# Recurrence, norms and the up-phase seam of a hybrid trunk layer: pinned program order, later scaling, other engines for some splits

## The chip, the core and the metric

The kernel is one program on one core of one Trainium2 chip. The core has five engines that run at once: TensorE (matmuls and transposes; PE in the profile, PEld its weight loads), VectorE (DVE), ScalarE (ACT), GpSimd (POOL) and SyncE (SP, which here only issues DMAs). The metric is device time of one execution in microseconds, as the median of three runs.

## The reference

One layer of a decoder trunk, for a sequence of 1024 tokens of width 1024, in float32:

```python
h = rms_norm(x, norm1_g); proj = h @ w_in
p_rwkv, p_sb, q_mem, gate_logits = split(proj)
y_a = rwkv7_branch(p_rwkv)        # 8 heads x 64: a recurrence over the tokens, then a norm per head
y_b = stick_breaking_branch(p_sb) # 8 heads x 64
y_m = memory_branch(q_mem, mem)   # 4 heads x 128
branch_out = einsum('btnc,ncd->btnd', stack(y_a, y_b, y_m), w_branch)
merged = sum_n sigmoid(gate_logits[n]) * branch_out[n]
x = x + merged @ w_out
x = x + conv_ffn(rms_norm(x, norm2_g))  # up (2 x 2816), causal conv of width 3, silu * value, down
```

In the recurrence each step does `S = S * w + (S @ -kk) (kk * a) + v k` and `y = S @ r`. The norm per head takes the mean and variance over the 64 channels of y.

## The kernel before

Every large product is made of three float32r matmuls: an operand is split into a high part (a rounding copy, on ScalarE) and a low part (operand minus high, on VectorE or GpSimd), and the product is high x high + high x low + low x high. `mm3` issues the three, `split_raw` makes the two parts of a weight (its low part on GpSimd, L81), `product` does the same for the up-projection.

Instructions are ordered on each engine by a scheduler, except where `pinned` is called while `self.pin` is set: `keep_in_program_order` puts such an instruction behind the instruction of the same engine that the code issued before it. TensorE's matmuls and transposes are all pinned there. Tiles come from pools with a fixed number of buffers, so a load into a new tile waits until the old tile's last reader is done.

The recurrence (`stage2`, about 812 to 1028 us) works in 16 chunks of 64 tokens, four pairs of heads each. A chunk has three steps, with a `yield` behind each: v1 from the state (copied from PSUM by VectorE, L527), w (copied by ScalarE, L535), and then y (ScalarE, L547, into the tiles `qk`) and the new state U (VectorE, L545; U and v1 share the tile `ys`). At each `yield` other work is woven in between: `gate_item`, the gates' projections (copied out by ScalarE at L745, multiplied by the row factor `rbc` on VectorE at L746), and `branch_item`, the branches' products (multiplied by the gate on VectorE at L1146, added to the merged tile on GpSimd at L1148, stored to `mrd` at L1149). `load_y` loads a branch's four input tiles (`yd`), and `split_y` splits them (L1108 high, L1109 low).

At each chunk step `next(norm)` also advances `norm_part`, the head norm of the chunks that are done: sums (L568), squares on ScalarE (L575, into the scratch tile `jk`), the power -1/2 on GpSimd (`rsqrt`, L165 and L166), and the scaling of y in pieces of 64 columns on VectorE (L582). `group_norm` then transposes y (`turn`, L596 and L597) and splits it. `branch_last` makes the last branch's product and the merged activations, `out_proj` multiplies them by `w_out` (eight tiles of tokens, `tt`), adds x and takes the second norm (`norm`), and transposes it (`spread`).

The feed-forward's up-projection is a Strassen-like product of quarters: `sums` makes differences of quarters (L1275), and seven products use the operands 11, 21, 22, T1, T2, T3 and T4, each split by `high` (L1288) and `low` (L1293). Weights come in pairs of blocks; `hl` splits a weight (L1377, L1378), `prep2` and `prep3` first make sums of weights on GpSimd (L1394 to L1407). The first pairs, from the output projection's last tile to about 1250 us, are the seam, whose order is written out by hand at the end of `up_phase`.

Of the kernel before, what the change touches and what calls it, by code (L numbers as in the profile page):

```python
# [49 lines left out]
class Trunk:  # L50
# [111 lines left out]
    def rsqrt(self, out, ss, n, scale, eps):  # L162
        nc = self.nc
        t = self.small("rs", [128, 16])
        nc.vector.tensor_scalar(t[:, :n], ss, scale, eps, ALU.mult, ALU.add)  # L165
        nc.gpsimd.tensor_tensor(out, t[:, :n], self.half[:, :n], ALU.pow)  # L166
# [305 lines left out]
    def stage2(self):  # L472
# [33 lines left out]
        for c in range(NC):  # L506
# [16 lines left out]
            for p, h2 in heads:  # L523
                _, _, _, M, wv, _, v1, pb = us[p]
                self.mmul(pb[hq[h2], A], M[hq[h2], h2 * 128 + 64 : h2 * 128 + 128], wv[h2][hq[h2]], start=(c == 0), stop=True)
                if h2 == 1:
                    nc.vector.tensor_copy(v1, pb[:, A])  # L527
# [11 lines left out]
            for p, (Up, ra, bt, M, wv, tt, v1, pb) in enumerate(us):  # L539
                for h2, q in enumerate(hq):  # L540
                    self.mmul(pb[q, Y], M[:, h2 * 128 : h2 * 128 + 64], wv[h2], start=(c == 0), stop=True)
                if c < NC - 1:
                    for h2, q in enumerate(hq):
                        self.mmul(pb[q, S], bt[:, q], wv[h2], start=True, stop=True)
                    nc.vector.scalar_tensor_tensor(Up, Up, self.pc[p][:, c : c + 1], pb[:, S], ALU.mult, ALU.add)  # L545
                for h2, q in enumerate(hq):
                    nc.scalar.activation(self.y[p][cc * 64 : cc * 64 + 64, g * 128 + h2 * 64 : g * 128 + h2 * 64 + 64], pb[q, Y], AF.Copy)  # L547
# [5 lines left out]
            if c in (3, 7, 11, 13, 15):  # L553
                for _ in norm:
                    pass
                norm = self.norm_part(*{3: (0, 2), 7: (2, 4), 11: (4, 6), 13: (6, 7), 15: (7, 8)}[c])
            if c == 13:
                self.gs = [self.load_gg(p) for p in range(2)]
        for _ in norm:
            pass  # L560

    def norm_part(self, g0, g1):
# [8 lines left out]
        groups = [[(y[:, j * 64 : (j + 1) * 64], p * nh + j) for j in range(nh)] for p, y in enumerate(ys)]  # L571
        for gs in groups:
            for y, j in gs:
                junk = self.small("jk", [128, 80], bufs=1)[:, :64]
                nc.scalar.activation(junk, y, AF.Square, bias=nm[:, j : j + 1], accum_out=vs[:, j : j + 1])  # L575
            yield
        rs = self.small("hf", [128, 16], bufs=4)
        self.rsqrt(rs[:, : 4 * nh], vs[:, : 4 * nh], 4 * nh, 1.0 / 64, 64e-5)
        yield
        for gs in groups:  # L580
            for y, j in gs:
                nc.vector.tensor_scalar(y, y, nm[:, j : j + 1], rs[:, j : j + 1], ALU.add, ALU.mult)  # L582
            yield

    def group_norm(self):
# [5 lines left out]
        def turn(p, h, eng):  # L591
# [5 lines left out]
            eng.tensor_tensor(y[:, hs], gg[:, hs], bg[:, hs], ALU.add)  # L597
# [7 lines left out]
        for p in range(4):  # L605
            turn(p, 0, nc.vector)
            if p % 2:
                yield
# [492 lines left out]
    def split_y(self, ys):  # L1101
        nc = self.nc
        hi = self.pool_a.tile([128, 4, 1024], F32R, name=self.nm("yhi"), tag="inst")
        his = [hi[:, k] for k in range(4)]
        out = []
        for hi, y in zip(his, ys):
            lo = self.t4("A", F32R)
            nc.scalar.activation(hi, y, AF.Copy)  # L1108
            nc.vector.tensor_tensor(lo, y, hi.bitcast(F32), ALU.subtract)  # L1109
            out.append((hi, lo))  # L1110
        return out

    def load_y(self, b):
        ys = []
        for k in range(4):
            y = self.t4("w4")
            self.nc.sync.dma_start(y, self.yd[b, k])
            ys.append(y)
        return self.split_y(ys)
# [5 lines left out]
    def branch_item(self, b, d, st, first):  # L1125
# [21 lines left out]
        if not first:  # L1147
            nc.gpsimd.tensor_tensor(g, g, o, ALU.add)  # L1148
# [3 lines left out]
    def branch(self, b, first):  # L1152
        st = {}

        def load():
            st["y"] = self.load_y(b)

# [5 lines left out]
        return load, items  # L1163
# [6 lines left out]
    def branch_last(self):  # L1170
# [7 lines left out]
        rest = []  # L1178
        for d in range(8):
            if d % 2 == 0:  # L1180
                w = self.split_w(self.I["w_br"][0, d // 2])
            g, o = self.t4("at"), self.t4()
            nc.sync.dma_start(g, self.gsd[0, d])
            nc.sync.dma_start(o, self.mrd[d])
# [10 lines left out]
            if d in (2, 3, 4, 5, 6):  # L1195
                self.load_wo(d - 2)
# [19 lines left out]
    def out_proj(self):  # L1216
        nc = self.nc
        for k in range(5, 8):
# [19 lines left out]
        def norm(tt, pp):  # L1238
# [9 lines left out]
            rs = self.small("rs2", [128, 1])  # L1248
            self.pinned(nc.vector.tensor_tensor(rs, ss[:, 0:1], ss[:, 1:2], ALU.add))
            self.rsqrt(rs, rs, 1, 1.0 / D, 1e-6)  # L1250
# [35 lines left out]
        def high(name, src, ts=slice(0, 512)):  # L1286
            for j in range(2):
                self.pinned(nc.scalar.activation(self.B[name][0][j][:, :, ts], src[j][:, :, ts], AF.Copy))  # L1288

        def low(name, src, eng, ts=slice(0, 512)):  # L1290
            for j in range(2):
                hi, lo = self.B[name][0][j][:, :, ts], self.B[name][1][j][:, :, ts]
                self.pinned(eng.tensor_tensor(lo, src[j][:, :, ts], hi.bitcast(F32), ALU.subtract))  # L1293

        def split(*a):
            high(*a[:2], *a[3:])
            low(*a)
# [4 lines left out]
        def late(tt):  # L1302
            spread(tt, sqs.pop(tt))
            if tt == 3:
                for i in (0, 1):
                    operand(("11", "21")[i], self.pool_l, "l4")
                    split(("11", "21")[i], [halves(j)[i] for j in range(2)], nc.gpsimd)
            elif tt == 5:
                sums(0, 256)
            elif tt == 6:  # L1310
                sums(256, 384)

# [26 lines left out]
        for tt in range(2, 8):  # L1339
# [4 lines left out]
            sqs[tt] = norm(tt, pp)  # L1344
            if tt == 5:
# [6 lines left out]
    def up_phase(self, raws, t2, operand, high, low, late, sums):  # L1352
        nc = self.nc
        old, new = slice(0, 384), slice(384, 512)
        operand("T2", self.pool_r, "T2", bufs=4)
        operand("T1", self.pool_l, "l4")
# [10 lines left out]
        def load(n):  # L1367
            if n < len(pairs):
                tag, m = ("rw", pairs[n][0]) if n % 2 == 0 else ("wr", pairs[n][0])
                pool = self.pool_r if n % 2 == 0 else self.pool_wt  # L1370
# [4 lines left out]
        def hl(src, pool, tags, n=1024):  # L1375
            hi, lo = (pool.tile([128, n], F32R, name=self.nm(t), tag=t, bufs=16 if t == "l4" else 2) for t in tags)
            nc.scalar.activation(hi, src, AF.Copy)  # L1377
            nc.gpsimd.tensor_tensor(lo, src, hi.bitcast(F32), ALU.subtract)  # L1378
# [7 lines left out]

        def prep2(n):
            if n == 0:
                w = self.early[1]
            else:  # L1390
# [500 lines left out]
```

## Time and profile before

| | |
|---|---|
| median of 3 runs | 1851.92 us (1851.91 to 1853.56) |
| the profiled execution | 1854.88 us, of which the span is 1853.1 us |
| mean granted TensorE clock | 0.992 |
| TensorE busy | 1793.0 us, 97% of the span |
| VectorE, ScalarE, GpSimd busy | 63%, 48%, 42% |

A row of the timeline gives the start, the length, the engine, the source line, what is written from what, and in square brackets the idle time of that engine before it with the event that ended it. A row of the windows gives for a stretch of time the busy time and count of each engine, then the clock that TensorE was granted, the share of DMA time and the GB/s.

### The profile page before, as it was taken

Reading aid. Unit: us, or ns where it says so; the run is one execution under the profiler, and the core shown is the slowest. Engines: PE = TensorE matmul, PEld = TensorE weight load, DVE = VectorE, ACT = ScalarE, POOL = GpSimd, SP = SyncE. Lnnn points to the kernel's source line nnn. Section 1 sums busy time; section 2 is a strip of 40 time slices with the busy share of each in tenths; the row PEclk is TensorE's granted clock in tenths of the full one; section 3 lists DMA queues with packets and bytes.
Section 4 is the critical chain, followed back from the end, with each engine's and each line's share of the span. In section 5 each row is a group of like instructions: output and inputs, shape, how many; then the busy total and the mean of one; then the engine's idle time right before and its main releaser. Section 6 shows DMA issues by size and latency. Waiting matters only on the chain. (4 is left out here: it accounts for less than half of the span.)

```text
span 1853.1 us, 27444 instructions
## 1 busy us (share of the span) xinstructions
PE 1793.0 (97%) x10468; PEld 1448.0 (78%) x10468; DVE 1171.0 (63%) x1654; ACT 880.9 (48%) x1665; POOL 783.6 (42%) x449
## 2 busy tenths in 40 slices
PE   8999999999999999998989999979999999999999
PEld 6777778878788887786767778768888888878877
DVE  5657664998987414323434682477776777885596
ACT  5443343555666635534536443454454444454433
POOL 2322343232222452112323350477776767545454
PEclk9999999999999999999999999999999999999999
DMA  4155465111112442558654462323232233395475
GB/s 179 58 170 182 160 205 183 49 42 53 52 53 76 123 129 78 180 207 274 215 188 179 174 235 103 114 68 108 93 123 92 95 116 108 120 324 204 142 243 189
DMA packets 120613, 263.39 MB, mean 142 GB/s; under 512 B 28313, under 2 KB 40857, under 8 KB 120354
## 3 DMA queue, kind: packets, MB, share of 16 engines
q1 hardware_dynamic: 82722, 194.76, 32.2%
q10 hardware_dynamic: 33984, 54.27, 8.0%
q0 software_dynamic: 3776, 12.62, 2.1%
q8 instruction: 82, 1.34, 0.3%
q14 instruction: 49, 0.40, 0.1%
HBM read 180.04 MB, written 81.53 MB: 141 GB/s over the span
## 5 line engine op out<-in xcount | busy, mean ns | idle before, releaser
L81 POOL TENSOR_TENSOR wl<-wr,wh 128x1024 fp32r<-128x1024 f32 x77 | 195.9, 2545 | 486.4 <-ACT wh L80 482.3
L112 PE MATMUL mm<-xhi,wh 128*128 128x512 f32 x784 | 265.8, 420 | 9.4 <-ACT xhi L179 7.5
L112 PE MATMUL mm<-xlo,wh 128*128 128x512 f32 x784 | 246.9, 396 | 0.9 <-DVE xlo L180 0.9
L112 PE MATMUL mm<-xhi,wl 128*128 128x512 f32 x784 | 244.6, 394 | 0.2 <-POOL wl L81 0.2
L112 PEld LDWEIGHTS mm<-xlo,wh 128*128 128x128 f32 x784 | 149.6, 191 | 35.1 <-DVE xlo L180 1.6
L112 PEld LDWEIGHTS mm<-xhi,wl 128*128 128x128 f32 x784 | 148.7, 190 | 34.4 <-POOL wl L81 1.1
L112 PEld LDWEIGHTS mm<-xhi,wh 128*128 128x128 f32 x784 | 138.5, 192 | 39.9 <-issue 9.1
L80 ACT ACTIVATE wh<-wr 128x1024 fp32r<-128x1024 f32 x77 | 81.4, 1057 | 144.6 <-PE mm L112 85.5
L112 PE MATMUL mm<-dw,da 128*128 128x512 f32 x528 | 121.5, 390 | 2.3 <-DVE da L1631 2.1
L112 PE MATMUL mm<-BT,l 128*128 128x512 f32 x504 | 117.9, 389 | 0.5 <-POOL l L1378 0.5
L112 PEld LDWEIGHTS mm<-dw,da 128*128 128x128 f32 x528 | 98.8, 188 | 24.3 <-DVE da L1631 3.4
L1632 POOL TENSOR_TENSOR dw<-draw,dw 128x512 fp32r<-128x512 f32 x55 | 81.4, 1488 | 83.5 <-ACT dw L1630 82.1
L112 PEld LDWEIGHTS mm<-BT,l 128*128 128x128 f32 x504 | 94.5, 188 | 20.5 <-POOL l L1378 1.0
L844 DVE TENSOR_TENSOR_SCAN at<-at,at 128x128 f32<-128x128 f32 (+3 forms) x64 | 93.3, 1459 | 26.6 <-ACT at L838 26.4
L112 PE MATMUL mm<-BT,wh 128*128 128x512 f32 x352 | 108.8, 390 | 0.7 <-DVE u L1430 0.7
L112 PE MATMUL mm<-B,wh 128*128 128x512 f32 x352 | 108.5, 389 | 0.0
L1631 DVE TENSOR_TENSOR da<-draw,da 128x512 fp32r<-128x512 f32 x77 | 65.7, 863 | 59.0 <-ACT da L1629 58.4
L112 PE MATMUL g<-dw,da 128*128 128x512 f32 x396 | 90.9, 390 | 2.2 <-ACT dw L1630 1.1
L1378 POOL TENSOR_TENSOR l<-it,l 128x1024 fp32r<-128x1024 f32 x21 | 50.8, 2418 | 92.3 <-ACT l L1377 92.3
L112 PEld LDWEIGHTS g<-dw,da 128*128 128x128 f32 x396 | 74.3, 188 | 18.4 <-ACT dw L1630 1.6
L1629 ACT ACTIVATE da<-draw 128x512 fp32r<-128x512 f32 x77 | 48.3, 628 | 83.3 <-PE mm L112 39.5
L746 DVE TENSOR_TENSOR w<-w,rbc 128x1024 f32<-128x1024 f32 x24 | 48.7, 2029 | 61.8 <-ACT w L745 61.8
(324 smaller groups left out, 3994.3 us busy)
## 6 DMA issues: line engine op xcount, KB each, us to landing
wr<-in_w_in_dram SPq DMA_DIRECT2D x50, 512.0 KB, 3.6
draw<-actd SPq DMA_DIRECT2D x77, 256.0 KB, 3.4
at<-scr SPq DMA_DIRECT2D x28, 512.0 KB, 6.4
draw<-in_w_down_dram SPq DMA_DIRECT2D x55, 256.0 KB, 4.7
wr<-in_w_up_dram SPq DMA_DIRECT2D x22, 512.0 KB, 3.4
actd<-gall ACTq DMA_DIRECT2D x44, 256.0 KB, 3.1
gsd<-w ACTq DMA_DIRECT2D x20, 512.0 KB, 2.8
rw<-in_w_up_dram SPq DMA_DIRECT2D x20, 512.0 KB, 3.6
```

The costliest lines, as they stand in the source:

```text
L80: self.nc.scalar.activation(hi, raw, AF.Copy)
L81: self.nc.gpsimd.tensor_tensor(lo, raw, hi.bitcast(F32), ALU.subtract)
L112: self.pinned(self.nc.tensor.matmul(*a, **k))
L746: nc.vector.tensor_tensor(g, g, self.rbc, ALU.mult)
L844: self.pinned(nc.vector.tensor_tensor_scan(sn[:, :W][:, ::-1], sn[:, :W][:, ::-1], self.smask[:, 1024 - W :][:, ::-1], 1.0, ALU.mult, ALU. ...
L1378: nc.gpsimd.tensor_tensor(lo, src, hi.bitcast(F32), ALU.subtract)
L1629: self.pinned(nc.scalar.activation(A[:, 0], a, AF.Copy))
L1631: self.pinned(nc.vector.tensor_tensor(A[:, 1], a, A[:, 0].bitcast(F32), ALU.subtract))
L1632: nc.gpsimd.tensor_tensor(Wt[:, 1], w, Wt[:, 0].bitcast(F32), ALU.subtract)
```

## The change

In the recurrence, the copies of v1, w and y, the state's update and the norm's squares and scalings become pinned. Squares come in batches of four, the scaling comes two or three steps later and in two halves, and the last part's norm goes on inside `group_norm`, where four more yields stand ahead of the second half of the turns. `load_y` asks for three tiles at once and for the fourth behind the first split, and each split is pinned at a step of the gate that follows. The last of the eight branch adds runs on VectorE. `branch_last` loads its gates one round earlier and begins `w_out` one round earlier. In `out_proj` the low part of 21 moves from GpSimd to VectorE one tile later, and T2's old columns are split there. In the seam the weights of pair two are loaded and summed first, T1 and T2 change pools, the low parts of 22 and of a weight move to VectorE, product 3 comes ahead of product 4, and the first pair's convolution moves into the second pair's loop.

The core of the diff:

```diff
-                    nc.vector.tensor_copy(v1, pb[:, A])
+                    self.pinned(nc.vector.tensor_copy(v1, pb[:, A]))
...
-                        nc.scalar.activation(w[q], pb[q, W], AF.Copy)
+                        self.pinned(nc.scalar.activation(w[q], pb[q, W], AF.Copy))
...
+                next(norm)
...
-        for _ in norm:
-            pass
+        for _ in range(3):
+            next(norm)
+        self.norm = norm
...
+        groups = [(y[:, j * 64 : (j + 1) * 64], p * nh + j) for p, y in enumerate(ys) for j in range(nh)]
+        for i in range(0, 4 * nh, 4):
+            for y, j in groups[i : i + 4]:
...
+                self.pinned(nc.scalar.activation(junk, y, AF.Square, bias=nm[:, j : j + 1], accum_out=vs[:, j : j + 1]))
             yield
...
+        for _ in range(0 if g0 == 7 else 3 if nh == 4 else 2):
+            yield
+        for i in range(2):
+            for y, j in groups[i * 2 * nh : (i + 1) * 2 * nh]:
+                self.pinned(nc.vector.tensor_scalar(y, y, nm[:, j : j + 1], rs[:, j : j + 1], ALU.add, ALU.mult))
             yield
...
+        for _ in range(4):
+            yield
         for p in range(4):
-            turn(p, 1, nc.vector)
+            turn(p, 1)
...
+        def first():
+            for _ in range(3):
+                load()
+        def split(k):
...
+            self.pinned(nc.scalar.activation(hi, y, AF.Copy))
+            self.pinned(nc.vector.tensor_tensor(lo, y, hi.bitcast(F32), ALU.subtract))
             out.append((hi, lo))
+            if k == 0:
+                load()
+        return first, {3 + k: functools.partial(split, k) for k in range(4)}
...
-            nc.gpsimd.tensor_tensor(g, g, o, ALU.add)
+            (nc.vector if d == 7 else nc.gpsimd).tensor_tensor(g, g, o, ALU.add)
...
-            if d in (2, 3, 4, 5, 6):
-                self.load_wo(d - 2)
+            if d in (1, 2, 3, 4):
+                self.load_wo(d - 1)
...
-                    split(("11", "21")[i], [halves(j)[i] for j in range(2)], nc.gpsimd)
+                    high(("11", "21")[i], [halves(j)[i] for j in range(2)])
+                low("11", [halves(j)[0] for j in range(2)], nc.gpsimd)
...
-            sqs[tt] = norm(tt, pp)
-            if tt == 5:
+            sqs[tt] = norm(tt, pp, split_t2 if tt == 7 else None)
+            if tt == 4:
+                low("21", [halves(j)[1] for j in range(2)], nc.vector)
...
         self.pin = True
+        load(1)
         prep1(0)
         prep1(1)
-        hi("T2", old)
         step(0, 1)
+        sums2(1)
+        hi("T1", old)
+        lo("T1", old)
         step(1, 1)
+        sums3(1)
         late(7)
+        hi("T3", old)
         sums(384, 512, (0,))
-        hi("22", old)
-        lo("22", old, nc.gpsimd)
-        lo("T2", old)
         hi("T2", new)
         lo("T2", new)
         sums(384, 512, (1,))
...
+        prep3(0)
+        hi("22", slice(0, 512))
+        lo("22", slice(0, 512))
...
         step(0, 7)
-        step(0, 4)
+        prep2(1)
+        u = step(0, 3)
+        prep3(1)
         load(2)
-        step(0, 3)
-        prep3(1)
+        v = step(0, 4)
         for n in range(1, len(pairs)):
-            order = (6, 5, 40, 7, 41, 3) if n == 1 else (1, 5, 6, 2, 7, 4, 3)
+            order = (6, 5, 7, 4, 3) if n == 1 else (1, 5, 6, 2, 7, 4, 3)
...
+                if n == 1 and i in (6, 5):
+                    conv(0, 1 if i == 6 else 0, v if i == 6 else u)
```

VectorE around chunk 6 of the recurrence, before (`A` is the low part of a tile of y's branch input, `qk` a tile of the head norm, `ys` holds U and v1, `g` is PSUM, `w` a gate or a merged tile):

```order
L582 TENSOR_SCALAR qk_6781<-qk_6781,hn_7571,hf_7848 128x64 x2
L1109 TENSOR_TENSOR A_7621<-w_1322_7609,yhi_7611 128x1024
L582 TENSOR_SCALAR qk_6781<-qk_6781,hn_7571,hf_7848 128x64 x2
L545 SCALAR_TENSOR_TENSOR ys_6782<-ys_6782,pc_90,g_7700 128x64
L545 SCALAR_TENSOR_TENSOR ys_6782<-ys_6782,pc_91,g_7701 128x64
L545 SCALAR_TENSOR_TENSOR ys_6782<-ys_6782,pc_92,g_7702 128x64
L545 SCALAR_TENSOR_TENSOR ys_6782<-ys_6782,pc_93,g_7703 128x64
L527 COPY ys_6782<-g_7852 128x64
L527 COPY ys_6782<-g_7853 128x64
L527 COPY ys_6782<-g_7854 128x64
L527 COPY ys_6782<-g_7855 128x64
L746 TENSOR_TENSOR w_1361_7844<-w_1361_7844,rbc 128x1024
```

and in the changed kernel:

```order
L1130 TENSOR_TENSOR A_7765<-w_1324_7613,yhi_7729 128x1024
L1130 TENSOR_TENSOR A_7774<-w_1325_7615,yhi_7729 128x1024
L548 SCALAR_TENSOR_TENSOR ys_6776<-ys_6776,pc_90,g_7693 128x64
L548 SCALAR_TENSOR_TENSOR ys_6776<-ys_6776,pc_91,g_7694 128x64
L548 SCALAR_TENSOR_TENSOR ys_6776<-ys_6776,pc_92,g_7695 128x64
L548 SCALAR_TENSOR_TENSOR ys_6776<-ys_6776,pc_93,g_7696 128x64
L1130 TENSOR_TENSOR A_7839<-w_1347_7733,yhi_7729 128x1024
L756 TENSOR_TENSOR w_1363_7848<-w_1363_7848,rbc 128x1024
L530 COPY ys_6776<-g_7852 128x64
L530 COPY ys_6776<-g_7853 128x64
L530 COPY ys_6776<-g_7854 128x64
L530 COPY ys_6776<-g_7855 128x64
```

Before, four v1 copies (L527) stand ahead of the gate's multiply by `rbc`; now that multiply, and the low part of the fourth tile of y ahead of it, stand in front of the copies (L530), and no scaling is left there.

GpSimd in the output projection, from the fourth tile's power to the first sums of up-weights, before (`rs` is the norm's factor, `B` a low part of 11 or 21):

```order
L166 TENSOR_TENSOR rs_1689_10329<-rs_10331,half 128x1
L1293 TENSOR_TENSOR B_1_0_10387<-raw_10008,B_0_0_10385 128x1024
L1293 TENSOR_TENSOR B_1_1_10388<-raw_10008,B_0_1_10386 128x1024
L1293 TENSOR_TENSOR B_1_0_10395<-raw_10008,B_0_0_10393 128x1024
L1293 TENSOR_TENSOR B_1_1_10396<-raw_10008,B_0_1_10394 128x1024
L166 TENSOR_TENSOR rs_1698_10428<-rs_10430,half 128x1
L1328 TENSOR_TENSOR wsum_10518<-wsec_10517 128x512
```

and in the changed kernel:

```order
L169 TENSOR_TENSOR rs_1689_10329<-rs_10331,half 128x1
L1318 TENSOR_TENSOR B_1_0_10387<-raw_10008,B_0_0_10385 128x1024
L1318 TENSOR_TENSOR B_1_1_10388<-raw_10008,B_0_1_10386 128x1024
L169 TENSOR_TENSOR rs_1698_10426<-rs_10428,half 128x1
L1355 TENSOR_TENSOR wsum_10518<-wsec_10517 128x512
L1356 TENSOR_TENSOR wsum_10518<-wsum_10518,at_10115 128x512
```

Two of the four splits between the two powers have left GpSimd.

VectorE at the start of the seam, before (`raw` and `A` hold quarters, `t` T2, `BT` a split operand, `p` a copied product):

```order
L1268 TENSOR_SCALAR A_10010<-g_10769,params 128x128 x2
L1268 TENSOR_SCALAR A_10012<-g_10778,params 128x128 x2
L1275 TENSOR_TENSOR raw_10008<-A_10009,raw_10008 128x2x128
L1275 TENSOR_TENSOR t_1652_10013<-A_10011,raw_10008 128x2x128
L1275 TENSOR_TENSOR raw_10008<-A_10010,raw_10008 128x2x128
L1275 TENSOR_TENSOR t_1653_10014<-A_10012,raw_10008 128x2x128
L1293 TENSOR_TENSOR BT_1_0_10722<-t_1652_10013,BT_0_0_10720 128x2x384
L1293 TENSOR_TENSOR BT_1_1_10723<-t_1653_10014,BT_0_1_10721 128x2x384
L1293 TENSOR_TENSOR BT_1_0_10722<-t_1652_10013,BT_0_0_10720 128x2x128
L1293 TENSOR_TENSOR BT_1_1_10723<-t_1653_10014,BT_0_1_10721 128x2x128
```

and in the changed kernel:

```order
L1318 TENSOR_TENSOR BT_1_0_10703<-t_1652_10013,BT_0_0_10701 128x2x384
L1272 TENSOR_TENSOR rs_1731_10715<-ss_1730_10709 128x1
L166 TENSOR_SCALAR rs_10718<-rs_1731_10715 128x1
L1318 TENSOR_TENSOR BT_1_1_10704<-t_1653_10014,BT_0_1_10702 128x2x384
L1508 COPY p_1736_10758<-mm_10745 128x512
L1318 TENSOR_TENSOR BT_1_0_10730<-raw_10008,BT_0_0_10728 128x2x384
L1318 TENSOR_TENSOR BT_1_1_10731<-raw_10008,BT_0_1_10729 128x2x384
L1508 COPY p_1739_10780<-mm_10767 128x512
L1293 TENSOR_SCALAR A_10010<-g_10785,params 128x128 x2
L1293 TENSOR_SCALAR A_10012<-g_10794,params 128x128 x2
L1300 TENSOR_TENSOR raw_10008<-A_10009,raw_10008 128x2x128
L1300 TENSOR_TENSOR t_1652_10013<-A_10011,raw_10008 128x2x128
```

The splits of T2's old columns (384 wide) now stand around the last tile's norm, and T1's old columns come next, ahead of the last differences; before, T2's four splits stood behind these differences.

More of the change, by code (lines that the diff above doesn't have):

```diff
@@ L1 @@
+import functools
 import itertools
@@ L1178, in branch_last, with load @@
         rest = []
+        go = {}
+        def load(d):
+            if d < 8:
+                go[d] = self.t4("at"), self.t4()
+                nc.sync.dma_start(go[d][0], self.gsd[0, d])
+                nc.sync.dma_start(go[d][1], self.mrd[d])
+        load(0)
         for d in range(8):
```

179 lines of the change are left out of this document (91 added, 88 removed).

## Prediction

> **What bounds the kernel now.** I read the page first, then every wait of TensorE in the timeline, then the clock by stretch, and last the engine that each wait names.
>
> ```profile
> PE 1793.0 (97%) x10468; PEld 1448.0 (78%) x10468; DVE 1171.0 (63%) x1654; ACT 880.9 (48%) x1665; POOL 783.6 (42%) x449
> ```
>
> TensorE is busy for 97% of the span. The change takes no matmul away, so all it can win are waits, and the half-speed matmuls behind long waits. These are the waits in the part of the program that it touches:
>
> ```profile
> 874.84 0.27 PE L112 MATMUL g<-ys,at 64*64 64x64 f32 x2 [3.11 <-ACT qk L547]
> 876.46 0.37 PE L112 MATMUL g<-ys,at 64*64 64x64 f32 x2 [0.81 <-ACT qk L547]
> 877.74 0.37 PE L112 MATMUL g<-ys,at 64*64 64x64 f32 x2 [0.80 <-ACT qk L547]
> 939.63 0.37 PE L112 MATMUL g<-ys,qk 64*64 64x64 f32 x2 [5.30 <-DVE ys L527]
> 994.48 0.27 PE L112 MATMUL g<-ys,qk 64*64 64x64 f32 x2 [1.52 <-DVE ys L527]
> 1004.04 0.27 PE L112 MATMUL g<-ys,it 64*64 64x64 f32 x2 [0.69 <-ACT qk L547]
> 1043.14 0.33 PE L105 MATMUL g<-kon,qk 128*128 128x128 f32 x1 [1.53 <-DVE qk L582]
> 1104.95 0.50 PE L112 MATMUL mm<-qk,mg 128*128 128x512 f32 x1 [1.54 <-DVE at L1199]
> 1171.11 0.33 PE L105 MATMUL g<-kon,w 128*128 128x128 f32 x1 [2.07 <-ACT w L1251]
> 1217.13 0.79 PE L112 MATMUL mm<-BT,wsh 128*128 128x512 f32 x1 [5.16 <-DVE BT L1293]
> 1232.57 0.50 PE L112 MATMUL mm<-B,l 128*128 128x512 f32 x1 [1.63 <-POOL l L1378]
> 1236.18 0.50 PE L112 MATMUL mm<-BT,l 128*128 128x512 f32 x1 [0.55 <-POOL l L1378]
> 1244.86 0.50 PE L112 MATMUL mm<-BT,wh 128*128 128x512 f32 x1 [0.69 <-DVE u L1430]
> 1249.48 0.47 PE L112 MATMUL mm<-B,l 128*128 128x512 f32 x1 [1.60 <-DVE u L1497]
> ```
>
> They add up to 27.0 us. Behind the three long ones the clock falls (PEclk is the sixth figure):
>
> ```profile
> 880.00:890.00 10.00, 10.00 (x91) 7.79 (x90) 7.05 (x22) 4.30 (x15) 2.43 (x1) 0.84 0.36 116
> 940.00:950.00 10.00, 10.00 (x87) 7.82 (x84) 2.07 (x9) 4.60 (x18) 0.01 (x1) 0.76 0.19 66
> 1210.00:1220.00 10.00, 4.84 (x16) 3.60 (x15) 9.96 (x12) 6.43 (x14) 6.63 (x5) 0.72 0.03 5
> 1220.00:1230.00 10.00, 10.00 (x41) 7.59 (x40) 8.90 (x14) 3.12 (x6) 5.40 (x2) 0.94 0.31 100
> ```
>
> Where TensorE is full, one minus the clock is work lost: 1.6 us behind 878, 2.4 behind 939, and behind 1217 half of 2.87 us plus 0.6, so 2.0. All that can go is therefore about 27.0 + 6.0 = 33 us. Elsewhere clock and order stay.
>
> **Part by part.** The wait at 939, in chunk 9 of the recurrence:
>
> ```profile
> 930.67 2.38 POOL L1148 TENSOR_TENSOR w<-w,w 128x1024 f32<-128x1024 f32 x1 [2.21 <-DMA w<-mrd]
> 933.94 2.93 POOL L166 TENSOR_TENSOR hf<-rs,half 128x16 f32<-128x16 f32 x1
> 936.90 2.54 DVE L582 TENSOR_SCALAR qk<-qk,hn,hf 128x64 f32<-128x64 f32 x11 [7.20 <-POOL hf L166]
> 939.36 0.61 DVE L527 COPY ys<-g 128x64 f32<-128x64 f32 x4
> ```
>
> The norm's power stands on GpSimd behind an add that waited for a load, and the scheduler put 11 scalings, which wait for that power, in front of the v1 copies that TensorE needs. The change delays the scaling by three yields and pins its two halves, so in the new order they follow copies that no longer depend on the power. Gain 5.30 + 2.4 = 7.7; nothing new is late there.
>
> The waits at 874 to 878, where chunk 5 needs chunk 4's y copies, and what follows:
>
> ```profile
> 873.26 1.06 ACT L1108 ACTIVATE yhi<-w 128x1024 fp32r<-128x1024 f32 x1 [3.58 <-DMA w<-yd]
> 874.34 0.92 ACT L547 ACTIVATE qk<-g 64x64 f32<-64x64 f32 x4
> 872.32 3.60 SPq L1117 DMA_DIRECT2D w<-yd  x2
> 879.10 0.32 SPq L1131 DMA_DIRECT2D w<-gsd  x1
> 879.53 1.06 ACT L1108 ACTIVATE yhi<-w 128x1024 fp32r<-128x1024 f32 x1 [1.04 <-DMA w<-yd]
> 884.93 1.22 DVE L1109 TENSOR_TENSOR A<-w,yhi 128x1024 fp32r<-128x1024 f32 x1
> 892.99 0.61 DVE L527 COPY ys<-g 128x64 f32<-128x64 f32 x4 [3.36 <-PE g L112]
> 894.06 2.41 DVE L746 TENSOR_TENSOR w<-w,rbc 128x1024 f32<-128x1024 f32 x1 [0.46 <-ACT w L745]
> ```
>
> A split that waited 3.58 us for y's second load stood ahead of the y copies. In the new order only the first split, whose load is long there, stands among them, with squares between single copies. I place the end of the last copy near 875.4 and the v1 copies near 876.7 instead of 879.0: gain 2.3, and about 0.5 of half clock.
>
> But y's third load now takes a slot that the store of a merged tile frees. The load that waited for that store in the old order went out at 879.10; the third load went out at 872.32 and landed after 7.2 us. With traffic down from there (DMA share 0.36) I allow 5 us: 884. Its two splits (1.06, 1.22) end near 886.4, and the fourth load, which waits for them, lands near 891 (4.6 us, an estimate from the same rows). Its splits, then the gate's multiply (2.41), stand in the new order ahead of chunk 6's v1 copies, which so cannot start before 896.9, not 892.99. TensorE reaches them near 892.8: a new wait of 4.1 us, and if the clock falls another 1.5. I charge 5.6; bounds are 0.5 (load in time) and 7 (load as slow as the old one). Net for this place: 2.8 - 5.6 = -2.8.
>
> The waits at 994 and 1004: the scaling leaves, but a gate multiply and a branch multiply stay ahead of copies. I place 2.5 us of waits for 2.2: -0.3. The wait at 1043 for the last part's scaling goes, since the second turn now comes four yields later: +1.5; 24 filler matmuls are its cover. The wait at 1104 stays: the load that it names stands on SP behind a weight load, and that behind the same split of w_out in the new order too: 0, at most +1.5.
>
> The output projection, 1171:
>
> ```profile
> 1159.92 9.46 POOL L1293 TENSOR_TENSOR B<-raw,B 128x1024 fp32r<-128x1024 f32 x4 [6.39 <-ACT B L1288]
> 1169.33 0.54 POOL L166 TENSOR_TENSOR rs<-rs,half 128x1 f32<-128x1 f32 x1
> ```
>
> The power waited for four splits. Two remain on GpSimd (to 1164.7); two go to VectorE around the small add, and the power can start near 1167.5. Some 0.3 us of the wait remain: +1.8.
>
> The seam, 1200 to 1250:
>
> ```profile
> 1198.24 0.43 DVE L1275 TENSOR_TENSOR t<-A,raw 128x256 f32<-128x256 f32 x1
> 1208.39 3.85 POOL L1293 TENSOR_TENSOR B<-A,B 128x768 fp32r<-128x768 f32 x2 [4.49 <-ACT B L1288]
> 1208.59 1.95 DVE L1275 TENSOR_TENSOR t<-A,raw 128x256 f32<-128x256 f32 x1
> 1212.20 2.52 POOL L1378 TENSOR_TENSOR wl<-wsec,wh 128x1024 fp32r<-128x1024 f32 x1
> 1214.93 2.48 DVE L1293 TENSOR_TENSOR BT<-t,BT 128x768 fp32r<-128x768 f32 x4
> 1228.74 1.30 POOL L1395 TENSOR_TENSOR it<-it,wr 128x512 f32<-128x512 f32 x1
> 1235.40 1.41 DVE L1440 SCALAR_TENSOR_TENSOR g<-u,params,g 128x512 f32<-128x512 f32 x2
> ```
>
> The small difference that takes 0.43 us alone takes 1.95 beside GpSimd, and its end follows the end of GpSimd's operation. [...]
>
> The old stall (5.16 + 2.0) is these differences and T2's four splits behind GpSimd's split of 22 and of a weight. The change splits T2's old columns in the output projection, takes the split of 22 and that weight from GpSimd, and gives it, a little earlier, four sums for pair two (1.30 each, 5.2 us, from about 1203.9). I place what is left from these rows:
> - T1's splits run into those sums, and the copy of product 1 of pair two comes late: 0.4.
> - T2's new columns end just behind their product's start: 0.3.
> - The split of the third weight is now VectorE's, behind an add and four splits of T3 (2.48 together): product 7 waits 1.3.
> - T4's two splits run beside GpSimd's splits of pair two's weights (2.4 us each): 0.9 and 1.1.
> - Pair one's convolution, twelve operations of 0.70, stands ahead of pair two's sum: 1.0.
>
> That is 5.0 for 5.16 + 2.0 + 1.63 + 0.55 + 0.69 + 1.60 = 11.6: +6.6. Without the two port waits it is +8.6; with them doubled, and one wait growing until the clock falls (3 more), +1.5. Product 3 ahead of 4 costs nothing itself: the same twelve matmuls change places.
>
> Sum: 7.7 - 2.8 - 0.3 + 1.5 + 0 + 1.8 + 6.6 = 14.5. The profiled execution took 1854.88 us and would take 1840.4; it lies 2.96 above the median of the runs, so against that median of 1851.92 it is 1837.4: **1837**.
>
> [...]
>
> **Rivals.**
> [...]
> - *VectorE becomes the bound of the seam.* It takes four splits more, and a fifth in the projection, while busy 9.96 of 10 us at 1210. The seam wins only 1.5, and chunk 6 loses 7 instead of 5.6: 14.5 - 5.1 - 1.4 = 8, so 1844. Against it: it gets T2 out of the way before 1205. [...]
> - *Slower: a pinned v1 copy stands behind a VectorE instruction with a late input, again and again.* In the old order the scheduler could let the copies pass; a pinned one cannot be passed. For it: in the new order a gate multiply is last ahead of these copies in four chunks, and halves of a scaling (eight of 0.23) in several more. One such place costs 5.6, as worked out for chunk 6. Each further one takes 5.6 from 14.5, so from the third on it is slower; with four, 1837.4 + 22.4 = 1860. Against it: three of those four stood there before, and of the waits there none was over 1.52.
> - *It does not do what it says.* Earlier loads still wait for the same slots, as in the last branch, and TensorE's order is nearly the same; gains and losses cancel: 1852.
>
> **Chances.** Forecast 0.50 (its own range 1832 to 1842); loads in time 0.17; VectorE the seam's bound 0.17; nothing 0.05; slower 0.11. A measurement of this kernel tells 0.2% (3.7 us) from no change. The first three are faster by more: 0.84; within: 0.05; slower: 0.11. The range leaves out the last two: from 1827 (the best ends of the 1104 wait and of the seam) to 1850 (the third case with chunk 9 only partly cured).
>
> **What would show it.** Right: no wait on v1 copies near 939 and full clock there; a wait near 893 on the v1 copies with a gate multiply just ahead of them, and the fourth load of y landing near 891; no 1.53 before the second turn; under 0.5 before the transposes at 1171; no wait over 3.4 us between 1200 and 1250, and full clock. Wrong: long waits of TensorE on v1 copies in chunks 10 to 15, or a wait over 3 us on a split of T1, T3 or T4, or the seam still at 1217 at half clock.

## Result and profile after

The changed kernel takes 1834.62 us (median of 6 runs, 1833.25 to 1839.12), the kernel before 1852.74 on the same chip (6 runs, 1851.42 to 1855.11): the ratio is 0.9906, 95% interval 0.9893 to 0.9919. The forecast was 1837, range 1827 to 1850. The profiled execution took 1834.23 us, with a span of 1832.5 and a mean granted clock of 0.997 (before 0.992).

The page's engine line of the changed kernel, then every wait of TensorE over 0.25 us in the changed part from its timeline (start, duration, instruction; in brackets the idle time before it and what ended it):

```profile
PE 1783.7 (97%) x10468; PEld 1442.8 (79%) x10468; DVE 1185.4 (65%) x1659; ACT 881.4 (48%) x1665; POOL 770.6 (42%) x441
...
871.48 0.33 PE L113 MATMUL g<-ys,at 64*64 64x64 f32 x4 [1.76 <-ACT qk L550]
872.63 0.33 PE L113 MATMUL g<-ys,at 64*64 64x64 f32 x4 [0.81 <-ACT qk L550]
893.17 0.87 PE L113 MATMUL g<-ys,qk 64*64 64x64 f32 x16 [3.00 <-DVE ys L530]
992.87 0.33 PE L113 MATMUL g<-ys,it 64*64 64x64 f32 x4 [0.70 <-ACT qk L550]
997.90 0.33 PE L113 MATMUL g<-ys,qk 64*64 64x64 f32 x4 [0.79 <-DVE ys L530]
1092.20 4.77 PE L113 MATMUL mm<-qk,mg 128*128 128x512 f32 x18 [1.53 <-DVE at L1220]
1195.54 0.73 PE L113 MATMUL mm<-B,wh 128*128 128x512 f32 x2 [1.47 <-DVE p L1508]
1205.62 0.49 PE L113 MATMUL mm<-BT,wl 128*128 128x512 f32 x1 [0.97 <-DVE wl L1409]
1212.33 0.50 PE L113 MATMUL mm<-BT,wh 128*128 128x512 f32 x1 [1.18 <-DVE BT L1318]
1215.65 0.50 PE L113 MATMUL mm<-BT,wh 128*128 128x512 f32 x1 [1.67 <-DVE BT L1318]
1229.05 2.97 PE L113 MATMUL mm<-B,l 128*128 128x512 f32 x12 [1.10 <-DVE u L1537]
```

They add up to 15.0 us instead of 27.0. The 5.30 at chunk 9, the 1.53 ahead of the second turn, the 2.07 at the projection and the 5.16 at the seam are gone; 893 is new, the three waits near 875 shrank from 4.72 to 2.57, and in the seam five short waits stand for the 5.16 and four short ones. The clock by stretch (PEclk is the sixth figure) is full in the stretches that answer to 939 and 1217; it falls at 873 and 893:

```profile
870.00:880.00 10.00, 7.70 (x59) 6.01 (x60) 2.03 (x6) 4.45 (x21) 2.93 (x1) 0.83 0.75 255
890.00:900.00 10.00, 7.00 (x77) 5.47 (x76) 4.08 (x11) 4.07 (x12) 0.43 (x1) 0.83 0.78 286
930.00:940.00 10.00, 10.00 (x97) 7.94 (x97) 1.47 (x8) 5.67 (x27) 4.40 (x3) 1.00 0.68 263
1210.00:1220.00 10.00, 7.15 (x31) 5.28 (x30) 9.04 (x8) 3.47 (x5) 9.92 (x6) 1.00 0.18 55
```

Three waits stand at the same work in all these traces and mark stages: 730 (line 1037), 1092 (line 1220) and 1629 (line 1678). In the timelines of before, then after:

```profile
730.29 1.98 PE L112 MATMUL mm<-at,A 128*128 128x512 f32 x4 [1.19 <-DVE qk L1027]
1649.38 2.79 PE L112 MATMUL mm<-dw,da 128*128 128x512 f32 x11 [1.38 <-DVE da L1631]
```

```profile
728.17 1.98 PE L113 MATMUL mm<-at,A 128*128 128x512 f32 x4 [1.18 <-DVE qk L1037]
1628.89 16.16 PE L113 MATMUL mm<-dw,da 128*128 128x512 f32 x70 [1.35 <-DVE da L1678]
```

With 1104.95 of before and 1092.20 of after, the recurrence's stage shrinks from 374.66 to 364.03 (10.63) and the projection and seam from 544.43 to 536.69 (7.74). The 2.12 us won before 730 are not the change's: before had two more half-clock stretches there, near 105 and 313 (3.41 us each, granted 0.50), at code that is the same, and the kernels of the experiments below reach the first mark anywhere from 728.09 to 730.62. So the change itself is worth 18.4 us in these two executions, close to the 18.1 between the medians. The listed waits account for 12.0 of it. About 4.1 more is the clock: between the first and the last mark TensorE worked at half clock (0.50 granted) for 15.1 us before and for 6.8 after, and half of that is lost. The remaining 2.3 us stand in no wait of the lists.

### The profile page after: what moved, and what is told of

It reads as the page before. It is cut to its first block, busy times and chain, and to the rows that moved or that the text cites. A ratio compares the mean times of both kernels' runs of the same rounds, so it can differ in the third digit from the quotient of the medians.

```text
span 1832.5 us, 27438 instructions
## 1 busy us (share of the span) xinstructions
PE 1783.7 (97%) x10468; PEld 1442.8 (79%) x10468; DVE 1185.4 (65%) x1659; ACT 881.4 (48%) x1665; POOL 770.6 (42%) x441
## 3 DMA queue, kind: packets, MB, share of 16 engines
q8 instruction: 82, 1.34, 0.3%
## 4 chain that ended last, share of the span: by engine, by line
PE 81%; DVE 10%; issue 4%; ACT 2%; POOL 2%; DMA 1%; ACTq 0%; SPq 0%; DVEq 0%; POOLq 0%
PE mm L113 65%; PE g L113 13%; PE g L106 3%; POOL dw L1679 1%; DVE at L854 1%; DVE it L462 1%; DVE qk L379 1%; DVE qk L381 1%; DVE inst L464 1%; DVE BT L1318 1%; DVE mg L1232 0%; DVE qk L817 0%; DMA at<-scr 0%; DVE g L1474 0%; ACT wh L81 0%
```

## Experiments

Each kernel's stages, worked out from the same three waits of its trace, beside its ratio to the kernel before:

| kernel | 730 to 1092 | 1092 to 1629 | ratio, 95% interval |
|---|---|---|---|
| before | 374.66 | 544.43 | 1 |
| changed | 364.03 | 536.69 | 0.9906 (0.9893 to 0.9919) |
| rec_only | 364.37 | 544.42 | 0.9950 (0.9938 to 0.9963) |
| seam_only | 374.17 | 536.80 | 0.9962 (0.9950 to 0.9973) |
| v1_free | 362.88 | 536.42 | 0.9902 (0.9889 to 0.9915) |
| y4_first | 361.58 | 536.70 | 0.9892 (0.9878 to 0.9906) |
| no_delay | 368.69 | 538.37 | 0.9924 (0.9912 to 0.9936) |
| scale_free | 365.74 | 536.82 | 0.9921 (0.9907 to 0.9934) |
| free_norm | 373.64 | 536.75 | 0.9957 (0.9941 to 0.9974) |
| port_act | 364.46 | 533.46 | 1 run |
| t4_pool | 364.64 | 535.56 | 0.9905 (0.9891 to 0.9919) |
| p_first | 364.07 | 536.26 | 1 run |
| lows_dve | 366.20 | 534.30 | 0.9899 (0.9884 to 0.9914) |
| combined | 365.63 | 535.90 | 0.9899 (0.9884 to 0.9914) |

The intervals are some 2.4 us to either side. By whole runs only rec_only, seam_only and free_norm differ clearly from the changed kernel; the others' intervals overlap with its own (port_act and p_first ran once), so single terms are read from the stages, of one trace each. How far a stage scatters can be read from the table too. Six kernels have the changed recurrence unaltered (changed, rec_only, port_act, t4_pool, p_first, lows_dve): 364.03 to 366.20, the last of them with one half-clock stretch more. Six have the changed seam unaltered (changed, seam_only, v1_free, y4_first, scale_free, free_norm): 536.42 to 536.82; no_delay has it too, and its 538.37 holds a half-clock stretch behind line 1220 (0.83 granted from 1095 to 1105).

**The two halves.** rec_only is the changed kernel with before's functions branch_last, out_proj and up_phase in place of its own; seam_only is before with these three and rsqrt taken from the changed kernel.

> The recurrence's part of the change alone (loading and splitting of y, pinned copies, squares and scalings, the delay, the second turn of the group norm); the last branch, the output projection and the seam are as before. Reading of the two traces: the start of chunk 15's v1 copies moved by 10.96 us, of which 2.12 stood before the changed part, and the spread transposes behind the group norm by 1.75 more, so 10.6 us should be won: about 1842. By the prediction's terms (7.7 - 2.8 - 0.3 + 1.5) it would be 6.1: about 1846.5. Rival: the two halves only work together (the stall that leaves the recurrence comes back in the old seam): under 4 us.

> The other half alone: the last branch, the output projection, the power's pinned addition and the seam are changed, the recurrence, y's loads and the group norm are as before. The two traces: about 2.1 us at the projection and 5.5 in the seam, 7.6 together: about 1845. By the prediction's terms (1.8 + 6.6) it is 8.4: about 1844.5. Rival that the halves interact: this and the recurrence alone do not add up to the 18.1 us of both.

The stages show 10.3 and 0.0 us for the one, 0.5 and 7.6 for the other: each half brings its own part and nothing in the other's stage, so the rival that they interact falls. By the ratios of whole runs they gave 9.3 and 7.0 us, 16.3 together for 17.4 of the whole change, within their intervals.

**Chunk 6: pin or load?** The timeline of the changed kernel (SyncE's queue, ScalarE, VectorE) shows what stands ahead of the v1 copies:

```profile
883.61 0.32 SPq L1118 DMA_DIRECT2D w<-yd  x1
888.23 1.06 ACT L1129 ACTIVATE yhi<-w 128x1024 fp32r<-128x1024 f32 x1 [1.39 <-DMA w<-yd]
889.33 1.22 DVE L1130 TENSOR_TENSOR A<-w,yhi 128x1024 fp32r<-128x1024 f32 x1 [4.98 <-ACT yhi L1129]
890.63 1.08 ACT L755 ACTIVATE w<-mm 128x512 f32<-128x512 f32 x2 [1.34 <-DMA qk<-vd]
891.75 1.23 DVE L756 TENSOR_TENSOR w<-w,rbc 128x1024 f32<-128x1024 f32 x1 [1.20 <-ACT w L755]
892.89 0.61 DVE L530 COPY ys<-g 128x64 f32<-128x64 f32 x4
```

```diff
-                    self.pinned(nc.vector.tensor_copy(v1, pb[:, A]))
+                    nc.vector.tensor_copy(v1, pb[:, A])
```

> The changed kernel, but the v1 copies aren't pinned; in chunk 6 the four copies then stand ahead of the fourth split of y and of the gate multiply; TensorE's order is the same. Theory (the prediction's step for chunk 6): TensorE's wait of 3.00 us on those copies is made by y's fourth load, whose split stands ahead of them, and by the gate multiply. It goes, and with it the half clock behind it (3.4 us at half speed, 1.7): 3.0 to 4.7 us less than the changed kernel, about 1830 to 1831.5. Rival: TensorE would wait there anyway, for the split itself or the next copies: within 1 us of the changed kernel.

```profile
888.56 0.62 DVE L530 COPY ys<-g 128x64 f32<-128x64 f32 x4 [2.58 <-PE g L113]
...
895.38 1.06 ACT L759 ACTIVATE w<-w 128x1024 f32<-128x1024 f32 x1 [1.29 <-DVE w L756]
896.83 1.86 ACT L538 ACTIVATE qk<-g 64x64 f32<-64x64 f32 x8 [0.40 <-ACT w L759]
897.33 1.27 PE L113 MATMUL g<-ys,at 64*64 64x64 f32 x12 [1.96 <-ACT qk L538]
```

In v1_free's timeline the copies run at once, but TensorE waits 1.96 us later for ScalarE, where the fourth split, the gate's copies and its sigmoid stand ahead of the next copies. The stage wins 1.15 us, not 3.0 to 4.7. Here the rival is nearer (TensorE waits for the next copies instead): unpinning one engine moved most of the wait to the other (3.00 us on VectorE, 1.96 on ScalarE). So the load itself was moved:

```diff
-            for _ in range(3):
+            for _ in range(4):
                 load()
...
-            if k == 0:
-                load()
```

> The changed kernel, but all four loads of y stand together, the fourth no longer behind the first split and behind two loads of the branch. In the kernel with free v1 copies the wait of 3.00 us in chunk 6 was not gone but had moved: 1.96 us on ScalarE's copies L538, which stood behind the fourth split, the gate's copies and its sigmoid, all late by that load. Theory: the load is the cause, whichever engine shows it. It is then issued near 876 instead of 883.6, lands before 884, and no wait over 1 us is left between 885 and 900, with full clock: 3.0 + 1.7 = 4.7 us less, about 1830. Rival: the slots that y's tiles free set the time, so the wait stays or goes over to the branch's loads, now behind it: within 1.5 us of the changed kernel.

```profile
878.43 0.80 SPq L1118 DMA_DIRECT2D w<-yd  x2
...
888.17 1.06 ACT L1129 ACTIVATE yhi<-w 128x1024 fp32r<-128x1024 f32 x1
...
891.69 2.14 DVE L756 TENSOR_TENSOR w<-w,rbc 128x1024 f32<-128x1024 f32 x1 [1.20 <-ACT w L755]
893.75 0.60 DVE L530 COPY ys<-g 128x64 f32<-128x64 f32 x4
894.02 0.72 PE L113 MATMUL g<-ys,qk 64*64 64x64 f32 x16 [1.34 <-DVE ys L530]
```

This trace reaches the first mark 2.45 us later than the changed kernel's (730.62 for 728.17), so its 893.75 answers to 891.30 there. The fourth split no longer waits for its load, the wait on the v1 copies falls to 1.34 us (2.92 to 3.87 in the six kernels with the same recurrence), the clock stays full behind it (pairs of 128x512 matmuls take 0.62 us from 895.24 on, as ahead of the wait), and the stage is 2.45 us shorter: the load is the main cause. By the distance between equal matmuls 3.2 us are won at chunk 6, and 0.7 are lost again near 929. What is left of the wait has two reasons in these rows: the split now stands in ScalarE's order behind the y copies, and the gate's multiply takes 2.14 us instead of 1.23, beside a split of a weight on GpSimd (890.26, 2.49 us).

**Chunk 9: what cured it?** In no_delay the empty steps ahead of the scalings go (the first edit), in scale_free the pin of the scalings (the second), in free_norm that of the squares as well (the second and the third).

```diff
-        for _ in range(0 if g0 == 7 else 3 if nh == 4 else 2):
+        for _ in range(0):
...
-                self.pinned(nc.vector.tensor_scalar(y, y, ..., ALU.add, ALU.mult))
+                nc.vector.tensor_scalar(y, y, ..., ALU.add, ALU.mult)
...
-                self.pinned(nc.scalar.activation(junk, y, AF.Square, ...))
+                nc.scalar.activation(junk, y, AF.Square, ...)
```

> The changed kernel, with the pinned scalings, but without the two or three empty steps ahead of them. The first eight scalings of the part after chunk 7 then stand, pinned, ahead of chunk 9's v1 copies. Theory: GpSimd's power, which starts at 932.4 and takes 2.93, holds them, and eight times 0.23 follow, so the copies start near 937.2 instead of 929.7: a wait of about 7.3 us on the v1 copies and half clock behind it (1.7): 7 to 10 us more than the changed kernel, about 1842 to 1845; one more if the other parts are late too. Rival: the pinning or the copies' order took the old wait away, not the delay: within 1 us of the changed kernel.

> The changed kernel, with the delay, but the scalings aren't pinned. The scheduler then puts sixteen of them right behind the power's addition, ahead of chunk 9's state updates, in the next part likewise, and eleven between y's first and second split. The kernel without the delay had no wait at chunk 9, so the delay is not what cured it. Theory: the pinning is. The power ends near 935.3, sixteen scalings take 3.7, so chunk 9's updates start near 939.1 instead of 937.6, and TensorE waits 1.5 us and up to 2.5 in the next part: 1 to 4 us more than the changed kernel. Prediction's step: a wait of the old size, 7.7. Rival: the copies' own pinning is enough: within 1 us.

> The changed kernel, with the delay and with pinned v1 copies, but neither the squares nor the scalings of the norm are pinned. VectorE's order at chunk 9 is then that of the kernel before: the power's addition, eleven scalings, the four v1 copies. TensorE's order is the same as in the changed kernel. Theory: what cured chunk 9 is that the pinned squares put the addition, and with it the scalings, behind the copies; so the wait returns: the power ends near 935.3, eleven scalings take 2.54, the copies start near 937.9 instead of 929.7: a wait of 5 to 8 us and half clock behind it, 7 to 10 us more than the changed kernel, 1842 to 1845. Rival: the load of the merged tile, late in the kernel before, comes in time now, and the wait stays under 2 us.

In the changed kernel the v1 copies of chunk 9 stand ahead of the power's addition (L166), on which the scalings hang:

```profile
929.70 0.61 DVE L530 COPY ys<-g 128x64 f32<-128x64 f32 x4 [3.35 <-PE g L113]
932.16 0.17 DVE L166 TENSOR_SCALAR rs<-hn 128x16 f32<-128x16 f32 x1 [1.84 <-ACT jk L580]
```

Before, that addition (929.53) and eleven scalings came first. no_delay's stage is 4.66 us longer, but not at chunk 9, where its timeline shows no wait. The scalings of the part before now stand ahead of chunk 6's copies, whose wait grows to 6.01 (and later ahead of chunk 10's, a wait of 1.17):

```profile
895.45 1.87 DVE L589 TENSOR_SCALAR qk<-qk,hn,hf 128x64 f32<-128x64 f32 x8
897.23 0.61 DVE L530 COPY ys<-g 128x64 f32<-128x64 f32 x4
897.50 1.12 PE L113 MATMUL g<-ys,qk 64*64 64x64 f32 x16 [6.01 <-DVE ys L530]
```

Both its theory and its rival missed the place. In scale_free too the copies (931.68) stand ahead of the addition (934.35); 16 scalings follow (937.58, 3.66 us), and there is no wait near 939. Its stage is 1.7 us longer, with a new wait of 0.96 us at chunk 10, but that is within the scatter of the stage. Only free_norm, with the delay and with pinned copies, brings the old wait back:

```profile
931.91 2.93 POOL L169 TENSOR_TENSOR hf<-rs,half 128x16 f32<-128x16 f32 x1
...
934.88 2.54 DVE L589 TENSOR_SCALAR qk<-qk,hn,hf 128x64 f32<-128x64 f32 x11 [6.54 <-POOL hf L169]
937.34 0.61 DVE L530 COPY ys<-g 128x64 f32<-128x64 f32 x4
...
937.60 1.12 PE L113 MATMUL g<-ys,qk 64*64 64x64 f32 x16 [4.73 <-DVE ys L530]
```

Its stage is 9.61 us longer than the changed kernel's, 6.7 of them at this place. scale_free and free_norm differ in nothing but the pin on the squares, and with it the wait goes. So the pinned squares cure chunk 9: in the three kernels that have them (changed, no_delay, scale_free) the addition comes behind the copies, also where the delay or the pin on the scalings is missing. The pin on the v1 copies is neither enough (free_norm has it) nor needed: v1_free has no wait there. Whether pinned scalings without pinned squares would do it too is not shown; that kernel was not run. The delay keeps the scalings out of chunk 6.

**The seam: GpSimd's splits or VectorE's order?** T4's two low parts beside GpSimd's splits of pair two, in the changed kernel's timeline:

```profile
1208.16 3.03 POOL L1409 TENSOR_TENSOR l<-it,l 128x1024 fp32r<-128x1024 f32 x1 [1.44 <-ACT l L1408]
1211.16 3.35 POOL L1409 TENSOR_TENSOR wl<-rw,wh 128x1024 fp32r<-128x1024 f32 x1
...
1208.86 6.73 DVE L1318 TENSOR_TENSOR BT<-raw,BT 128x1024 fp32r<-128x1024 f32 x2
```

t4_pool gives T4's low parts to GpSimd (the first edit); lows_dve gives the two splits to VectorE behind T4's (the second); p_first puts step(1, 1) ahead of T1's old parts (the third); port_act leaves the two low parts out and lets ScalarE write copies in their place, so its product is another one (the fourth).

```diff
-        lo("T4", slice(0, 512))
+        lo("T4", slice(0, 512), nc.gpsimd)
```

```diff
-            ... fixed=n < 2) if n else self.early[1]
+            ... fixed=n < 2, eng=nc.vector if n == 1 else nc.gpsimd) if n else self.early[1]
-            ... eng=nc.gpsimd if n else nc.vector)
+            ... eng=nc.gpsimd if n > 1 else nc.vector)
```

```diff
+        step(1, 1)
         hi("T1", old)
         lo("T1", old)
-        step(1, 1)
```

```diff
+            if eng is None:
+                keep(nc.scalar.activation(lo, src, AF.Copy))
...
+            ... fixed=n < 2, eng=None if n == 1 else nc.gpsimd) ...
+            ... eng=nc.vector if n == 0 else None if n == 1 else nc.gpsimd)
```

> The changed kernel, but GpSimd's two splits of pair two's weights (the low parts of the sum and of the second weight) are left out: ScalarE writes copies in their place, so the output is another one. [...] Rival: T4's splits are long by themselves (four matrices in fp32r, or fed by late high parts): they stay over 5 us.

> The changed kernel, but T4's two low parts go to GpSimd, ahead of its splits of pair two's weights. [...] 1.5 to 2.9 us less, about 1832. Rival: GpSimd is then the bound, and pair two's products 6 and 7 wait for its splits what product 4 no longer waits: within 1 us.

> The changed kernel, but the two splits of pair two's weights that ran on GpSimd beside T4's go to VectorE, behind T4's, where it waits for TensorE. [...] Rival: VectorE is the bound there, so two splits more delay pair one's convolution and pair two's sum: within 1 us.

> The changed kernel, but pair two's product 1, and with it VectorE's copy of it, stands ahead of T1's two old low parts; the copy is done near 1191 instead of 1195.5, and TensorE's wait of 1.47 us on it goes. [...] Rival (the wait itself costs): the seam is 1.0 to 1.5 us shorter.

T4's low parts in port_act and in lows_dve, one row each from their timelines:

```profile
1209.32 3.45 DVE L1318 TENSOR_TENSOR BT<-raw,BT 128x1024 fp32r<-128x1024 f32 x2
```

```profile
1212.96 2.35 DVE L1318 TENSOR_TENSOR BT<-raw,BT 128x1024 fp32r<-128x1024 f32 x2
```

Beside one of GpSimd's sums (2.19 us) the two take 3.45 us, with GpSimd idle 2.35, not 6.73: the rival that they are long by themselves falls. In both kernels the waits of 1.18 and 1.67 are gone. The stage is 3.23 us shorter in port_act and 2.39 in lows_dve, where VectorE takes 2.35 us for two splits of 1024 columns and GpSimd 2.41 and 2.40 for one each, in rows of line 1409 further on. Added up, T4's two and GpSimd's two are 7.16 us; in the changed kernel they took 7.43 from the first start to the last end, so side by side on the two engines they took no less than that sum. In lows_dve 0.45 us came back on one of the moved splits, and pair one's convolution holds TensorE for 1.36 us instead of 1.10. In t4_pool the trouble changes sides:

```profile
1208.55 6.04 POOL L1318 TENSOR_TENSOR BT<-raw,BT 128x1024 fp32r<-128x1024 f32 x2 [1.23 <-DVE B L1318]
...
1210.24 2.10 DVE L1533 TENSOR_TENSOR u<-u 128x512 f32<-128x512 f32 x1
```

An addition that took 0.68 in port_act took 2.10, GpSimd needed 6.04 for the two splits, and the stage won only 1.13, less than the 1.5 to 2.9 that were expected. In p_first the 1.47 went, and 0.49 and 0.19 came back on T2's high and low part. The stage is 0.43 shorter, hardly more than the scatter, so most of the gain on that wait was lost behind it. That agrees with VectorE having no time to spare there, but rests on one trace.

**Both together.** combined has y4_first's loads, lows_dve's splits, and one more empty step between the second and third group of squares, one less ahead of the scalings.

```diff
             yield
+            if i == 4 and nh == 4:
+                yield
...
-        for _ in range(0 if g0 == 7 else 3 if nh == 4 else 2):
+        for _ in range(0 if g0 == 7 else 2):
```

> The changed kernel with three changes: the four loads of y together, the two splits of pair two's weights on VectorE, and the squares' last two groups one step later (so that only twelve stand ahead of chunk 4's last y copies, one empty step less behind them). By the parts: 2.4 us in chunk 6 (364.03 to 361.58 between the wait at 728 and the one at 1092, as the kernel with the four loads together showed), 2.3 to 3.3 in the seam, and of the waits of 1.76 and 0.81 and the half clock behind them (1.7) 2 to 4: 7 to 9.5 us less, about 1825 to 1828. Rival: four squares then stand ahead of chunk 5's y copies and give the wait back there: 5 us less, about 1830.

Neither the 7 to 9.5 us nor the rival's 5 came. At 871 the wait shrank to 0.61 and the one at 893 went, but at 990 to 998 TensorE waits 1.21, 1.75 and 0.99 us in place of 0.70 and 0.79, with half clock behind them, and there is a half-clock stretch behind the wait on line 1220 (0.83 granted from 1095 to 1105). By the distance between equal matmuls 4.9 us were won at chunks 5 and 6 and 6.2 lost from 988 to 1004. Its ratio cannot be told from that of the changed kernel. If the gains of y4_first and lows_dve add up, the two without the moved squares would be 4.8 us below the changed kernel (361.58 and 534.30); that kernel was not run.

## Why the forecast held, term by term

TensorE runs the same matmuls in nearly the same order, so the distance between equal matmuls of the two traces gives each term, from one wait-free place to the next:

| place | forecast | measured |
|---|---|---|
| chunks 5 and 6 | -2.8 | -0.7 |
| chunk 9 (939) | +7.7 | +7.65 |
| 994 and 1004 | -0.3 | +2.0 |
| second turn (1043) | +1.5 | +1.7 |
| 1104 | 0 | 0.0 |
| projection (1171) | +1.8 | +2.2 |
| seam | +6.6 | +5.5 |
| sum | 14.5 | 18.4 |

The gain came out 3.9 us above the sum, and inside the range. Chunks 5 and 6 are off by 2.1 and the place at 994 by 2.3 us in one direction, the seam by 1.1 in the other, so the sum hides a part of the misses.

- *Chunk 9.* Right in size, since the whole old wait and its half clock went; the reason was half right. It was put on the delay and the pinned scalings. The copies do pass ahead, but no_delay shows no wait here without the delay and scale_free none without the pin on the scalings; free_norm shows that the pin on the squares does it.
- *Chunks 5 and 6.* The mechanism was right, its size too dear. The first place won 3.95 instead of 2.8: 2.15 in the listed waits, about the 2.3 placed, and most of the rest by the clock, where only 0.5 was placed. Half clock there went from 6.83 us to 3.41; before, it began at 876.4, ahead of the row of 880 from which it was read. The new wait came where it was placed, with the gate's multiply just ahead of the copies. It was 3.00 instead of 4.1, because the gate's multiply took 1.23 with GpSimd idle, not 2.41, and the half clock cost 1.7 for 1.5. What failed in part is the place: the pin on the v1 copies was blamed, and v1_free shows that ScalarE's order carries the same load onto TensorE.
- *994 and 1004.* The term that was mis-signed: 0.70 and 0.79 are left where 2.5 was placed, so a gate multiply ahead of pinned copies cost at most 0.79 there. The waits, with three of 0.14 before, explain 1.15 of the 2.0; the other 0.8 lies in stretches that the timeline shows as busy, and its cause stays open.
- *Seam.* 6.39 us of waits remain instead of 5.0. The copy of product 1 was the mis-sized one (1.47 for 0.4: the two T1 splits took 3.95 us beside GpSimd's sums, the row below); T4's are 1.18 and 1.67 for 0.9 and 1.1, the third weight 0.97 for 1.3, pair one's convolution 1.10 for 1.0, T2 none for 0.3. No run shows the port that the seam's ends of 8.6 and 1.5 speak of; the runs show what T4's two splits take beside the other engine's work: 6.73 us in the changed kernel, 2.35 in lows_dve, 6.04 on GpSimd in t4_pool. Nor does one show 3.4 us as a limit for waits: half clock came behind the 3.00 at 893 too, and the seam's longest wait is 1.67.

```profile
1190.94 3.95 DVE L1318 TENSOR_TENSOR BT<-raw,BT 128x768 fp32r<-128x768 f32 x2 [0.77 <-ACT BT L1313]
```

- *Rivals.* The slower one, pinned copies held again and again, happened in chunk 6 alone. VectorE's own work is not the seam's bound: lows_dve gave it two splits more and the stage shrank by 2.39. What holds the seam in part is the time that VectorE and GpSimd take from each other (T4's two splits 6.73 us instead of 2.35), without half clock (1.00 granted from 1200 to 1230). The loads were not in time: the fourth split still waited 1.39 us for its own.
- *Range.* The lower end of 1827 does not come out of the ends that it names: with 1.5 more at 1104 and 2.0 more in the seam the 14.5 become 18.0, which gives 1833.9, and with the load of chunk 6 in time (5.1 more) 1828.8.

## What to carry to other kernels

The late load showed here on whichever engine stood in order behind it: unpinning the engine that the wait names moved most of the wait (3.00 us became 1.96 elsewhere), loading earlier shortened it (to 1.34). Where two engines hold each other up, as VectorE and GpSimd do here (two splits took 6.73 us instead of 2.35), count what an operation takes from both, and give it to the engine on which it is shorter (here a split of 1024 columns took 1.2 us on VectorE, 2.4 on GpSimd), in a gap of that engine. Read a small edit from the stage between two waits that both traces share, not from the span, since elsewhere stretches of half clock, 1.7 us lost in each 3.41, came and went in these traces (ahead of 730 before had three, the changed kernel one). Even then compare it with the scatter of stages whose code is the same.

## What was not expected of the hardware

Up to 1800 us the granted clock is 0.50 in six stretches of before and in three of the changed kernel, each 3.41 us long or twice that, and 1.00 between them (start and length in us):

| kernel | half clock from | length | waits of TensorE just ahead of it or at its start (their end) |
|---|---|---|---|
| before | 105.0 | 3.41 | 2.26 (103.57) |
| before | 272.3 | 3.41 | 2.55 (270.79) |
| before | 313.2 | 3.41 | none on record from 300 on |
| before | 876.4 | 6.83 | 3.11 (874.84), 0.81 (876.46) |
| before | 937.9 | 6.83 | 5.30 (939.63) |
| before | 1214.4 | 6.83 | 5.16 (1217.13) |
| changed | 269.0 | 3.41 | 2.57 (269.14) |
| changed | 873.1 | 3.41 | 1.76 (871.48), 0.81 (872.63) |
| changed | 893.6 | 3.41 | 3.00 (893.17) |

The length of a single wait did not tell: the clock stayed at 1.00 behind the 2.07 at 1171 of before, and fell behind the 1.76 and 0.81 of the changed kernel and, at 313 of before, with no wait on record ahead. So a wait of 1.53 cost nothing in one trace and 1.7 us in another; after, then no_delay, the wait on line 1220 and its clock:

```profile
1090.00:1100.00 10.00, 8.37 (x36) 6.34 (x36) 10.00 (x12) 4.18 (x8) 5.34 (x2) 1.00 0.17 52
```

```profile
1098.17 6.14 PE L113 MATMUL mm<-qk,mg 128*128 128x512 f32 x17 [1.53 <-DVE at L1220]
...
1095.00:1105.00 10.00, 8.36 (x29) 6.18 (x28) 10.00 (x12) 3.85 (x6) 5.38 (x3) 0.83 0.20 62
```

What decides it was not shown.
